# First mixer of a two-layer diffusion block: TensorE in a written order, each head's core in steps inside the next head's projection, scores in 32-wide pieces, conditioning ends put later

## Chip, cores and metric

One core of one Trainium2 chip. The metric is the device time of one execution in microseconds. TensorE does the matmuls (its weight loads are listed apart as PEld), VectorE (DVE) and ScalarE (ACT) work element by element, GpSimd (POOL) does a few small things, SyncE (SP) only issues transfers.

## What is computed

Two layers over 256 context and 256 latent tokens of width 1024. Each layer is a mixer and a mixture of 32 experts, both modulated by shifts, scales and gates that come from a conditioning vector. The first layer's mixer is a gated linear recurrence with 8 heads of 128, run forward and backward in chunks; the second's is attention. Cut to the part at hand:

```python
def gla_chunkwise(q, k, v, log_f, s0):          # per head, chunks of 32
    def step(s, blk):
        qc, kc, vc, gc = blk
        b = jnp.cumsum(gc, axis=-2)
        q_dec = qc * jnp.exp(b)
        scores = jnp.einsum('bhtc,bhsc->bhts', q_dec, kc * jnp.exp(-b))
        scores = jnp.where(lower_tri, scores, 0.0)
        o = scores @ vc + q_dec @ s             # and s_new from kc * exp(b_end - b), vc
    ...
def hgrn2_mixer(h_lat, h_ctx, ...):
    p = h @ w_in                                # q, z_fw, z_bw, v, g of 1024 each
    f = lb + (1 - lb) * sigmoid(z);  k = 1 - f;  log_f = log(f)
    ...                                         # context first, then latents; and both flipped
    return (rms_norm(o_fw + o_bw) * silu(g)) @ w_out

mod = silu(c) @ ada_w[i] + ada_b[i]             # six chunks of 1024: the conditioning
```

## The kernel before

The kernel is written in Python over a library that builds each engine's instruction list. Where nothing else is said, that library's planner sets the order on every engine: it takes the program's order as priority, its own cost estimate of each instruction and the buffers that come free, and puts on an engine what is ready. Inside a manual block for an engine, that engine keeps the order of the program; the others are still planned. Each engine then runs its list in order; waits between engines are semaphores.

`hgrn` (from L267) is the first mixer. All 512 tokens stand transposed as `hH` and `hL`, a high and a low part in a reduced fp32 format, so that a product of full precision is three matmuls. Weights arrive by SyncE in 2 MB (`slot`), are parted by `split` (L259) into `wH` (a ScalarE cast) and `wL` (a VectorE subtraction), three buffers each.

- Values (`vproj`, L378; `vstep`, L279): for heads 0 to 3 and again for heads 4 to 7, 96 matmuls into four accumulators; ScalarE copies them to `V4`. The second time is at head 4.
- Projections of a head (L506 to L523): four outputs q = 0 to 3 of 24 matmuls of 512 columns each (L513 to L515), one accumulator each: the two directions' gates, the query, the output gate. `dir_pre` (L393) turns a gate into `eq`, `ek`, `ke`, `kx` and `e` by a chain over ScalarE and VectorE with a scan; queries and output gates go through `sigmoid` (L176) and a product (L521).
- Conditioning: `ada_some(4)` (L373) puts four pieces behind each of the first six heads. A piece (`ada_piece`, L206) loads 1 MB of weights by SyncE into one of two buffers and multiplies it in four side-by-side 32-wide parts of the array (L212). Behind every eighth piece comes an end: the bias row, four transposes through the bank `sm` (L225), copies, and four small transfers by GpSimd (L242).
- Core of a head (`core`, L431): per direction `qm` and `qt` on VectorE, the scores (L450 with `ek`, 32 wide at a place of the array; L454 with `kx`, 64 wide), a masked copy (L456), three transposes of `ke` (L465), their copy `kT` on ScalarE (L467), three state products (L471), `S` (L473, L475); then the output (L487) of 20 instructions, its square sums, its norm (L494), four transposes (L498) and the gate (L499).

PSUM has eight banks: four rotating accumulators `mm` (projections, conditioning, router), one bank `sm` for all transposes and state products, one for the output, two for the scores. The order in the program is: the head's projection, its conditioning pieces, its core; the planner places the core's matmuls among the next head's projection. Behind head 7 come the router's small products (L606), the output projection (L558) and the routing; then the experts, whose weights (2 MB each) stream through the slots on SyncE's queue (L1029, L1032). The second layer's mixer, `mla`, runs sixteen more conditioning pieces by the same `ada_piece`.

Of the kernel before, what the change touches and what calls it, by code (L numbers as in the profile page):

```python
# [82 lines left out]
class K:  # L83
# [122 lines left out]
    def ada_piece(self, l, g, k, ps, w, tmp):  # L206
        nc, I = self.nc, self.I
        nc.sync.dma_start(w, I["ada_w"][l, g, k])
        if k == 0:
            self.ada_ps = ps()  # L210
        for a in range(4):
            nc.tensor.matmul(self.ada_ps[a * 32:(a + 1) * 32, :], self.cS[:, k, :], w[:, a * 512:(a + 1) * 512],  # L212
                             start=(k == 0), stop=(k == 7))
        if k < 7:
            return
        b, S, gf = tmp()
        (nc.scalar if l else nc.sync).dma_start(b, I["ada_b"][l, g])
        nc.vector.tensor_tensor(S, self.ada_ps, b, op=ALU.add)
        if g == 2:
            gf = gf[0:64]  # L220
            (nc.scalar if l else nc.sync).dma_start(gf, I["gffn"][l])
            nc.vector.scalar_tensor_tensor(S[0:64], S[0:64], 1.0, gf, op0=ALU.add, op1=ALU.mult)
# [44 lines left out]
    def hgrn(self):  # L267
        tc, nc, I = self.tc, self.nc, self.I
        PE, V, S, G = nc.tensor, nc.vector, nc.scalar, nc.gpsimd
        with ExitStack() as left, ExitStack() as st:  # L270
# [8 lines left out]
            def vstep(acc, k, H, L):  # L279
                c = slice(k % 2 * 512, k % 2 * 512 + 512)  # L280
                for tt in range(4):
                    ts = slice(tt * 128, tt * 128 + 128)
                    PE.matmul(acc[tt], hH[:, k, ts], H[:, c], start=(k == 0), stop=False)
                    PE.matmul(acc[tt], hH[:, k, ts], L[:, c], start=False, stop=False)
                    PE.matmul(acc[tt], hL[:, k, ts], H[:, c], start=False, stop=(k == 7))

            with tc.tile_pool(name="hin", bufs=1, side="right", reuse_waits="tile") as ip:
# [36 lines left out]
                for k in range(8):  # L324
                    if k % 2 == 0:
                        H, L = self.split(raw[:, k * 512:k * 512 + 1024], wp, [128, 1024])
                    vstep(acc, k, H, L)
# [41 lines left out]

            ada_todo = [(0, 1, k) for k in range(8)] + [(0, 2, k) for k in range(8)]  # L370
# [6 lines left out]

            def vproj(i, V4):  # L378

                acc_ = acc  # L380
                if i:
                    acc_, raw = [self.mm() for _ in range(4)], self.slot()
                    nc.sync.dma_start(raw, I["hg_wv"][i])
                    for q in range(4):
                        H, L = self.split(raw[:, q * 1024:(q + 1) * 1024], wp, [128, 1024])
                        for k in (2 * q, 2 * q + 1):
                            vstep(acc_, k, H, L)
                for tt in range(4):
                    S.copy(V4[:, tt, :], acc_[tt])

            v4 = lambda t: t.rearrange("p (t c j) -> p t c j", t=4, c=2)

            def dir_pre(h, d, z):  # L393
# [29 lines left out]
                ke = cw.tile([128, 512], F32, tag="ke", name="ke", bufs=2)  # L423
# [6 lines left out]

            def core(h, V4, hh, dd, sq, gs, dst):  # L431
                vs = slice(hh * 128, hh * 128 + 128)
                Sst, qts, scs = [], [], []
                both = cw.tile([128, 512], F32, tag="on", name="both")
                for d in range(2):
                    x = dd[d]
                    qm = x["eq"]
                    V.tensor_tensor(qm, sq, x["eq"], op=ALU.mult)
                    qt = cw.tile([128, 512], F32, tag="qt", name="qt", bufs=2)
                    V.tensor_tensor(v4(qt), v4(qm), x["sq"].to_broadcast([128, 4, 2, 64]), op=ALU.mult)  # L440
# [3 lines left out]
                    psc = scP[d]  # L444
                    for tt in range(4):
                        a = tt * 128
                        for c in range(4):
                            s0, c0 = a + c * 32, a + (c // 2) * 64
                            t0, n = (c0, 64) if c % 2 == d else (s0, 32)
                            PE.matmul(psc[c * 32:c * 32 + 32, t0:t0 + n], x["ek"][:, s0:s0 + 32], qm[:, t0:t0 + n],  # L450
                                      start=True, stop=True, tile_position=(0, c * 32))

                        t0 = a + 64 * (1 - d)
                        PE.matmul(psc[d * 64:d * 64 + 64, t0:t0 + 64], x["kx"][:, tt, :], qm[:, t0:t0 + 64], start=True, stop=True)  # L454
                    sc = scT[d]
                    V.copy_predicated(sc.rearrange("p (t j) -> p t j", t=4), masks[d].to_broadcast([128, 4, 128]),  # L456
                                      psc.rearrange("p (t j) -> p t j", t=4))
                    scs.append(sc)
                    if d:
                        V.tensor_tensor(both, scs[0], sc, op=ALU.add)  # L460
                    order = [0, 1, 2, 3] if d == 0 else [1, 0, 3, 2]
# [5 lines left out]
                    S.copy(kT, pk[:, 0:384])  # L467
                    pd = self.sm()
# [8 lines left out]
                    Sst.append((ss, {order[i + 1]: i for i in range(3)}))  # L477
                po = self.ac()
# [11 lines left out]
                for tt in range(4):  # L490
# [4 lines left out]
                                ssq.rearrange("p (t o) -> p t o", o=1).to_broadcast([128, 4, 128]), op=ALU.mult)  # L495
                pt = self.sm()
# [4 lines left out]
            for h in range(8):  # L501
                if h % 4 == 0:
                    V4 = cw.tile([128, 4, 512], F32, tag="V4", name="V4", bufs=2)
                    vproj(h // 4, V4)
# [3 lines left out]
                for q in range(4):  # L508
                    H, L = self.split(raw[:, q * 1024:(q + 1) * 1024], wp, [128, 1024])
                    p = self.mm()  # L510
                    for k in range(8):
# [3 lines left out]
                        PE.matmul(p, L[:, c], hH[:, k, :], start=False, stop=(k == 7))  # L515
                    if q < 2:
                        dd.append(dir_pre(h, q, p))
                    else:
# [3 lines left out]
                        if q == 2:  # L522
                            sq = t  # L523
                        else:
                            gs = t
                if h < 6:
                    ada_some(4)
                o7 = []

                def dst():  # L530
# [4 lines left out]
                if h == 5:  # L535
                    self.load_router(hp, 0)
                if h == 7:
                    self.router(hp, 0, self.mm())
                core(h, V4, h % 4, dd, sq, gs, dst)


# [991 lines left out]
```

## Time and profile before

| | us |
|---|---|
| runs of the kernel before | 1577.63, 1576.82, 1574.11 (median 1576.82) |
| the profiled execution | 1578.04 |
| its span, first to last instruction | 1576.3 |
| TensorE busy | 1499.6 (95%) |
| VectorE, ScalarE busy | 813.2 (52%), 449.1 (28%) |
| projections of heads 0 to 7, start to end | 53.1 to 344.7 |

The busy time of an engine is the time in which at least one of its instructions is under way. Matmuls are pipelined: a row's own duration reaches into the next one's, so a matmul's cost in a stream is the distance between two starts. The granted clock (PEclk) is the share of 2.4 GHz that TensorE was given; one half is 1.2 GHz.

### The profile page before, as it was taken

What the parts mean: (1) busy time and instruction counts of PE and PEld (TensorE: products, weight loads), DVE (VectorE), ACT (ScalarE), POOL (GpSimd) and SP (SyncE); (2) the same over time, 40 slices, a digit from 0 to 9 for tenths busy, and PEclk for the clock granted to TensorE, in tenths of its full rate; (3) what the DMA queues carried; (4) which work ended last, traced back from release to release, by engine and by line L of the source; (5) the groups of instructions that cost most, each with busy time, mean ns of one, the idle gap of its engine ahead of it and who ended that gap; (6) DMA issues with size and microseconds to landing.
All of it is one profiled execution on the core that took longest, in us unless ns stands there. A gap on an engine that the chain in (4) does not pass through costs nothing. (4 is left out here: it accounts for less than half of the span.)

```text
span 1576.3 us, 20139 instructions
## 1 busy us (share of the span) xinstructions
PE 1499.6 (95%) x8009; PEld 825.2 (52%) x8010; DVE 813.2 (52%) x1675; ACT 449.1 (28%) x938; POOL 74.9 (5%) x101
## 2 busy tenths in 40 slices
PE   7999999999899999999999999989799999998997
PEld 4777787778644544544544454447444443433433
DVE  5776647775824544544544567674534332332333
ACT  4554445553411111111111145554411111111110
POOL 0000000001300000000000011310100000000000
PEclk9999999999799999999999999999899999999999
DMA  9454534414769999999999957344799999999997
GB/s 384 165 201 177 196 136 161 188 54 161 276 240 399 429 428 426 428 427 426 427 429 423 356 218 305 141 187 142 272 392 428 427 427 428 428 427 428 427 425 268
DMA packets 63127, 500.80 MB, mean 318 GB/s; under 512 B 7024, under 2 KB 16624, under 8 KB 32816
## 3 DMA queue, kind: packets, MB, share of 16 engines
q1 hardware_dynamic: 59296, 490.87, 76.5%
q10 hardware_dynamic: 2816, 7.26, 1.4%
q0 software_dynamic: 912, 1.27, 0.3%
q8 instruction: 67, 1.10, 0.3%
q14 instruction: 36, 0.29, 0.0%
HBM read 498.26 MB, written 1.11 MB: 317 GB/s over the span
## 5 line engine op out<-in xcount | busy, mean ns | idle before, releaser
L1038 PE MATMUL mm<-w,xT 128*64 128x512 f32 x2048 | 469.9, 595 | 19.8 <-DMA w<-in_wg_dram 16.4
L1038 PEld LDWEIGHTS mm<-w,xT 128*64 128x64 f32 x2048 | 146.8, 137 | 310.7 <-issue 266.3
L1089 DVE TENSOR_TENSOR tmp<-p,rG 128x512 f32<-128x512 f32 (+1 forms) x106 | 68.0, 644 | 132.7 <-PE p L1087 132.6
L1090 DVE TENSOR_TENSOR x<-x,tmp 128x512 f32<-128x512 f32 (+1 forms) x195 | 132.4, 679 | 6.7
L1089 DVE TENSOR_TENSOR tmp<-p,x 128x512 f32<-128x512 f32 (+1 forms) x68 | 44.4, 655 | 165.1 <-PE p L1087 165.1
L1069 PE MATMUL mm<-w,x 128*64 128x512 f32 (+1 forms) x544 | 116.3, 570 | 1.6 <-ACT x L1057 1.4
L1069 PE MATMUL mm<-w,hT 128*64 128x512 f32 (+1 forms) x544 | 113.9, 570 | 1.4 <-ACT hT L1057 1.4
L889 PE MATMUL p<-sel,h2H 128*128 128x256 f32 x384 | 101.8, 300 | 1.8 <-DVE sel L879 1.8
L513 PE MATMUL mm<-hH,wH 128*128 128x512 f32 x256 | 101.9, 398 | 0.3 <-ACT wH L262 0.3
L515 PE MATMUL mm<-hH,wL 128*128 128x512 f32 x256 | 101.3, 396 | 0.5 <-DVE wL L264 0.5
L514 PE MATMUL mm<-hL,wH 128*128 128x512 f32 x256 | 100.6, 393 | 0.0
L890 PE MATMUL p<-sel,h2L 128*128 128x256 f32 x384 | 98.5, 290 | 0.0
L1076 DVE SCALAR_TENSOR_TENSOR yL<-mm,wsl,yH 128x512 fp32r<-128x512 f32 (+1 forms) x68 | 48.7, 716 | 71.6 <-ACT yH L1075 71.6
L1075 ACT ACTIVATE yH<-mm,wsl 128x512 fp32r<-128x512 f32 (+1 forms) x68 | 45.1, 663 | 123.3 <-PE mm L1069 93.2
L889 PEld LDWEIGHTS p<-sel,h2H 128*128 128x128 f32 x384 | 76.7, 200 | 5.1 <-issue 2.4
L264 DVE TENSOR_TENSOR wL<-w,wH 128x1024 fp32r<-128x1024 f32 x55 | 67.0, 1221 | 23.5 <-ACT wH L262 22.0
L1086 PE MATMUL p<-yH,G 128*128 128x512 f32 (+1 forms) x174 | 76.2, 441 | 0.9 <-DVE tmp L1089 0.9
L890 PEld LDWEIGHTS p<-sel,h2L 128*128 128x128 f32 x384 | 76.3, 199 | 1.4 <-issue 0.8
L1069 PEld LDWEIGHTS mm<-w,x 128*64 128x64 f32 x544 | 45.6, 137 | 60.0 <-issue 45.6
L262 ACT CAST wH<-w 128x1024 fp32r<-128x1024 f32 x55 | 57.3, 1047 | 63.3 <-PE mm L514 32.8
L1069 PEld LDWEIGHTS mm<-w,hT 128*64 128x64 f32 x544 | 37.5, 137 | 65.8 <-issue 59.7
L1086 PEld LDWEIGHTS p<-yH,G 128*128 128x128 f32 x174 | 32.5, 187 | 65.8 <-issue 51.5
(392 smaller groups left out, 2119.2 us busy)
## 6 DMA issues: line engine op xcount, KB each, us to landing
w<-in_wg_dram SPq DMA_DIRECT2D x52, 2048.0 KB, 18.1
w<-in_wu_dram SPq DMA_DIRECT2D x52, 2048.0 KB, 21.4
w<-in_wd_dram SPq DMA_DIRECT2D x52, 2048.0 KB, 20.2
aw<-in_ada_w_dram SPq DMA_DIRECT2D x32, 1024.0 KB, 6.0
w<-in_wd_dram SPq DMA_DIRECT2D x48, 512.0 KB, 8.7
w<-in_hg_w_dram SPq DMA_DIRECT2D x8, 2048.0 KB, 7.9
w<-in_wg_dram SPq DMA_DIRECT2D x32, 512.0 KB, 7.8
w<-in_wu_dram SPq DMA_DIRECT2D x32, 512.0 KB, 9.5
```

The lines of the kernel that those rows point to most:

```text
L262: nc.scalar.copy(H, raw)
L264: nc.vector.tensor_tensor(L, raw, H, op=ALU.subtract)
L513: PE.matmul(p, H[:, c], hH[:, k, :], start=(k == 0), stop=False)
L514: PE.matmul(p, H[:, c], hL[:, k, :], start=False, stop=False)
L515: PE.matmul(p, L[:, c], hH[:, k, :], start=False, stop=(k == 7))
L889: self.nc.tensor.matmul(o, self.h2H[:, tt, c], r, start=(tt == 0 and k == 0), stop=False)
L890: self.nc.tensor.matmul(o, self.h2L[:, tt, c], r, start=False, stop=(last and k == 1))
L1038: PE.matmul(p[a * 64:(a + 1) * 64, :], xT[:, k, a * 64:(a + 1) * 64], ws[a][:, k * 512:(k + 1) * 512], start=(k == 0), stop=(k == 7))
L1069: PE.matmul(p[a * 64:(a + 1) * 64, :], hT[:, j, a * 64:(a + 1) * 64], ws[a][:, j * 1024 + n * w_:j * 1024 + n * w_ + w_], start=(j == 0), ...
L1086: PE.matmul(pc, g, yH, start=True, stop=False)
L1089: V.tensor_tensor(t, pc, rG[vec(tt)][:, ns], op=ALU.mult)
L1090: adder.tensor_tensor(x[:, tt, ns], x[:, tt, ns], t, op=ALU.add)
```

## The change

TensorE gets a manual block over the loop of the heads. Projections, value projection and core become generators; `beside` runs a projection in 32 steps of three matmuls and takes the next step of the previous head's core behind steps 7, 10, 12, 17, 19, 22 and 30. Conditioning pieces come in pairs behind steps 7 and 21; an end that is left over comes behind step 5 of the next job. The scores of both directions come together, and the `kx` products are cut from 64 to 32 wide. `ke` has three buffers in place of two. The bias row is asked for at piece 5 (in the second layer's later groups at piece 5 and again at piece 7).

```diff
@@ ada_piece
+        if k == 5 or (l == 1 and g and k == 7):
+            self.ada_tmp = b, S, gf = tmp()
+            (nc.scalar if l else nc.sync).dma_start(b, I["ada_b"][l, g])
+            if g == 2:
+                (nc.scalar if l else nc.sync).dma_start(gf[0:64], I["gffn"][l])
         if k < 7:
             return
-        b, S, gf = tmp()
-        (nc.scalar if l else nc.sync).dma_start(b, I["ada_b"][l, g])
+        b, S, gf = self.ada_tmp
         nc.vector.tensor_tensor(S, self.ada_ps, b, op=ALU.add)
...
+        if l == 1 and g:
+            self.ada_tail(l, g, S)
+        else:
+            self.ada_left = l, g, S
+
+    def ada_tail(self, l, g, S):
...
@@ vstep
                     PE.matmul(acc[tt], hL[:, k, ts], H[:, c], start=False, stop=(k == 7))
+                    yield
...
-                ke = cw.tile([128, 512], F32, tag="ke", name="ke", bufs=2)
+                ke = cw.tile([128, 512], F32, tag="ke", name="ke", bufs=3)
...
+            def scores(dd, qms):
+                for tt in range(4):
+                    a = tt * 128
+                    for d in range(2):
+                        for c in range(4):
+                            s0, c0 = a + c * 32, a + (c // 2) * 64
+                            t0, n = (c0, 64) if c % 2 == d else (s0, 32)
+                            PE.matmul(scP[d][c * 32:c * 32 + 32, t0:t0 + n], dd[d]["ek"][:, s0:s0 + 32], qms[d][:, t0:t0 + n],
+                                      start=True, stop=True, tile_position=(0, c * 32))
+                    for c in range(4):
+                        d = c // 2
+                        t0 = a + 64 * (1 - d)
+                        PE.matmul(scP[d][c * 32:c * 32 + 32, t0:t0 + 64], dd[d]["kx"][:, tt, c % 2 * 32:c % 2 * 32 + 32],
+                                  qms[d][:, t0:t0 + 64], start=True, stop=True, tile_position=(0, c * 32))
+
+            def core(h, V4, dd, sq, gs, dst):
+                for d in range(2):
+                    qm = dd[d]["eq"]
+                    V.tensor_tensor(qm, sq, qm, op=ALU.mult)
+                    qms.append(qm)
+                yield
+                scores(dd, qms)
+                ...             # qt, masked copies, both
+                for d in range(2):
+                    yield
+                    ...         # transposes of ke, kT
+                    yield
+                    ...         # state products, S
+                yield
+                ...             # output, square sums, norm
+                yield
+                ...             # four transposes, gate
...
-                        PE.matmul(psc[d * 64:d * 64 + 64, t0:t0 + 64], x["kx"][:, tt, :], qm[:, t0:t0 + 64], start=True, stop=True)
...
+            def beside(job, side, ada=False):
+                next(side, None)
+                for i, _ in enumerate(job, 1):
+                    if i == 5 and self.ada_left:
+                        self.ada_tail(*self.ada_left)
+                        self.ada_left = None
+                    if ada and i in (7, 21):
+                        ada_some(2)
+                    if i in (7, 10, 12, 17, 19, 22, 30):
+                        next(side, None)
+
+            V4, side = values(acc), iter(())
+            with tc.manual_schedule(engines={mybir.EngineType.PE}):
+                for h in range(8):
+                    if h == 4:
+                        res = []
+                        beside(vproj(res), side)
+                        V4, side = res[0], iter(())
+                    res = []
+                    beside(project(h, res), side, h < 6)
+                    side = core(h, V4, *res, dst_of(h))
+                    if h == 5:
+                        self.load_router(hp, 0)
+            self.router(hp, 0, self.mm())
+            for _ in side:
+                pass
```

## Rows read from the trace of the kernel before

**Rows 1.** The page: busy time of the engines, and the span in 40 equal slices (39.4 us each), busy share in tenths, for TensorE and for the transfers.
```profile
PE 1499.6 (95%) x8009; PEld 825.2 (52%) x8010; DVE 813.2 (52%) x1675; ACT 449.1 (28%) x938; POOL 74.9 (5%) x101
...
PE   7999999999899999999999999989799999998997
...
DMA  9454534414769999999999957344799999999997
```
**Rows 2.** Busy time of each engine by stretches: the projections of heads 0 to 7, the last head of them, the tail of the mixer, and most of the first expert stage. Columns: stretch, its length, then busy us and instructions of TensorE, its weight loads, VectorE, ScalarE and GpSimd, the granted clock, the transfers' share and GB/s.
```profile
53.13:344.68 291.55, 289.57 (x1922) 216.47 (x1922) 203.39 (x376) 151.74 (x301) 5.77 (x22) 1.00 0.42 159
313.35:346.25 32.90, 31.99 (x233) 25.56 (x234) 25.14 (x48) 18.98 (x39) 0.04 (x1) 1.00 0.17 65
346.25:412.14 65.89, 62.08 (x363) 50.54 (x364) 42.42 (x93) 24.76 (x50) 13.64 (x15) 0.95 0.39 134
480.00:900.00 420.00, 419.32 (x2083) 194.79 (x2081) 202.35 (x323) 45.79 (x83) 0.00 (x0) 1.00 1.01 422
```
**Rows 3.** TensorE's timeline around the end of head 1's projection: start, duration, line, operation, result and operands, weights' and moving shapes, count. Between the first two rows lie 67 more projection matmuls; the conditioning matmuls (L212), the scores (L450, L454) and the next projection follow.
```profile
95.63 0.39 PE L513 MATMUL mm<-hH,wH 128*128 128x512 f32 x1
...
111.06 0.39 PE L515 MATMUL mm<-hH,wL 128*128 128x512 f32 x1
111.38 1.92 PE L212 MATMUL mm<-aw,cS 128*32 128x512 f32 x16
113.12 0.29 PE L450 MATMUL p<-eq,ek 128*32 128x64 f32 x8
113.34 0.33 PE L454 MATMUL p<-eq,kx 128*64 128x64 f32 x2
113.59 0.31 PE L450 MATMUL p<-eq,ek 128*32 128x64 f32 x8
...
117.13 0.50 PE L513 MATMUL mm<-hH,wH 128*128 128x512 f32 x1
...
119.53 0.39 PE L514 MATMUL mm<-hL,wH 128*128 128x512 f32 x1
119.84 1.07 PE L212 MATMUL mm<-aw,cS 128*32 128x512 f32 x8
120.84 0.49 PE L487 MATMUL p<-V,both 128*128 128x128 f32 x2
121.08 0.47 PE L515 MATMUL mm<-hH,wL 128*128 128x512 f32 x1
121.40 0.39 PE L513 MATMUL mm<-hH,wH 128*128 128x512 f32 x1
```
**Rows 4.** The 64-wide score matmuls of the window from 53.13 to 344.68 us, grouped by line and shape: count, busy us together, mean ns of one, idle time before them.
```profile
L454 PE MATMUL p<-eq,kx 128*64 128x64 f32 x112 | 18.4, 246 | 0.0
```
**Rows 5.** Timelines of TensorE, ScalarE and VectorE over the core of head 5 (transposes, copy, state products, the two copies and updates of the state, output, the projection that goes on behind it, cast of the next weights, transposes).
```profile
321.74 0.49 PE L465 MATMUL p<-ident,ke 128*128 128x128 f32 x3
...
322.79 0.94 PE L471 MATMUL p<-V,kT 128*128 128x128 f32 x6
...
324.08 0.49 PE L487 MATMUL p<-S,qt 128*128 128x128 f32 x2
...
326.12 0.48 PE L513 MATMUL mm<-hH,wH 128*128 128x512 f32 x1
...
331.40 0.63 PE L498 MATMUL p<-ident,on 128*128 128x128 f32 x4
...
322.26 0.48 ACT L467 COPY kT<-p 128x384 f32<-128x384 f32 x1 [3.04 <-PE p L465]
...
327.77 1.03 ACT L262 CAST wH<-w 128x1024 fp32r<-128x1024 f32 x1
...
324.06 0.73 DVE L475 SCALAR_TENSOR_TENSOR S<-S,e,p 128x128 f32<-128x128 f32 x2 [2.14 <-ACT S L473]
```
**Rows 6.** Timelines of TensorE, VectorE and ScalarE where head 3's projection ends and the second value projection (L283) begins; L521 is the last reader of the fourth projection accumulator, L182 one of the three ScalarE steps of the sigmoid before it.
```profile
183.24 1.92 PE L212 MATMUL mm<-aw,cS 128*32 128x512 f32 x16
...
188.99 0.50 PE L283 MATMUL mm<-wH,hH 128*128 128x512 f32 x1
...
188.72 0.68 DVE L521 TENSOR_TENSOR sq<-sq,mm 128x512 f32<-128x512 f32 x1
...
186.49 0.63 ACT L182 ACTIVATE sq<-sq 128x512 f32<-128x512 f32 x1
```
**Rows 7.** Transfers: the conditioning weights on SyncE's queue (count, size, median us from issue to landing), and the bias rows of the second layer on ScalarE's (duration of an issue in ns, least, median and most, first and last start).
```profile
aw<-in_ada_w_dram SPq DMA_DIRECT2D x32, 1024.0 KB, 6.0
...
L217 ACTq DMA_DIRECT2D w<-in_ada_b_dram x2: 338/343/348, 933.5 to 968.9; - x2
```
**Rows 8.** Waits of SyncE's queue from 340 to 480 us: who waited for whom, us in total, times, longest.
```profile
SPq L1029 <- DVE wL L264: 75.4, 2, 43.4
```
**Rows 9.** All engines' timeline at the start of a conditioning pair (weight loads and matmuls of L212), and the weight loads of the `ek` products from 53.13 to 344.68 us by shape.
```profile
111.38 0.16 PEld L212 LDWEIGHTS mm<-aw,cS 128*32 128x32 f32 x8 [0.35 <-issue]
111.38 1.06 PE L212 MATMUL mm<-aw,cS 128*32 128x512 f32 x8
...
111.83 0.13 PEld L212 LDWEIGHTS mm<-aw,cS 128*32 128x32 f32 x4 [0.30 <-issue]
...
L450 PEld LDWEIGHTS p<-eq,ek 128*32 128x32 f32 x448 | 9.2, 108 | 8.8 <-DVE eq L438 4.0 <-issue 1.6 <-DVE ke L428 0.3
```
**Rows 10.** Waits in the window from 53.13 to 344.68 us: the casts of weights that waited for TensorE to leave a buffer.
```profile
ACT wH L262 <- PE mm L514: 32.8, 15, 9.4
```

More of the change, by code (lines that the diff above doesn't have):

```diff
@@ L326, in hgrn @@
                         H, L = self.split(raw[:, k * 512:k * 512 + 1024], wp, [128, 1024])
-                    vstep(acc, k, H, L)
+                    for _ in vstep(acc, k, H, L):
+                        pass
             self.dump("hT", hH)
@@ L376, in ada_some, with values, vproj @@
                                    lambda: [hp.tile([128, 512], F32, tag="adx", name=f"ad{t}", bufs=4) for t in "bsg"])
[L378 to L387, printed above, removed]
+            def values(acc_):
+                V4 = cw.tile([128, 4, 512], F32, tag="V4", name="V4", bufs=2)
                 for tt in range(4):
                     S.copy(V4[:, tt, :], acc_[tt])
+                return V4
+            def vproj(res):
+                acc_, raw = [self.mm() for _ in range(4)], self.slot()
+                nc.sync.dma_start(raw, I["hg_wv"][1])
+                for q in range(4):
+                    H, L = self.split(raw[:, q * 1024:(q + 1) * 1024], wp, [128, 1024])
+                    for k in (2 * q, 2 * q + 1):
+                        yield from vstep(acc_, k, H, L)
+                res.append(values(acc_))
             v4 = lambda t: t.rearrange("p (t c j) -> p t c j", t=4, c=2)
@@ L429, in dir_pre @@
                 return dict(eq=eq, ek=ek, ke=ke, kx=kx, sq=sq_, E=e)
-            def core(h, V4, hh, dd, sq, gs, dst):
-                vs = slice(hh * 128, hh * 128 + 128)
-                Sst, qts, scs = [], [], []
+            def scores(dd, qms):
[13 more added lines that the diff above has]
+            def core(h, V4, dd, sq, gs, dst):
+                vs = slice(h % 4 * 128, h % 4 * 128 + 128)
+                orders = [[0, 1, 2, 3], [1, 0, 3, 2]]
+                Sst, qts, qms = [], [], []
+                for d in range(2):
[4 more added lines that the diff above has]
+                scores(dd, qms)
                 both = cw.tile([128, 512], F32, tag="on", name="both")
@@ L436, in core @@
                     x = dd[d]
-                    qm = x["eq"]
-                    V.tensor_tensor(qm, sq, x["eq"], op=ALU.mult)
                     qt = cw.tile([128, 512], F32, tag="qt", name="qt", bufs=2)
-                    V.tensor_tensor(v4(qt), v4(qm), x["sq"].to_broadcast([128, 4, 2, 64]), op=ALU.mult)
+                    V.tensor_tensor(v4(qt), v4(qms[d]), x["sq"].to_broadcast([128, 4, 2, 64]), op=ALU.mult)
                     second = v4(qt)[:, :, 1 - d, :]
@@ L443, in core @@
                     qts.append(qt)
[L444 to L453, printed above, removed]
-                        PE.matmul(psc[d * 64:d * 64 + 64, t0:t0 + 64], x["kx"][:, tt, :], qm[:, t0:t0 + 64], start=True, stop=True)
[L455 to L461, printed above, removed]
+                for d in range(2):
+                    V.copy_predicated(scT[d].rearrange("p (t j) -> p t j", t=4), masks[d].to_broadcast([128, 4, 128]),
+                                      scP[d].rearrange("p (t j) -> p t j", t=4))
+                V.tensor_tensor(both, scT[0], scT[1], op=ALU.add)
+                for d in range(2):
+                    x, order = dd[d], orders[d]
+                    yield
                     pk = self.sm()
@@ L499, in core, with project @@
                 V.scalar_tensor_tensor(dst(), pt, self.cols[:, 64:65], gs, op0=ALU.mult, op1=ALU.mult)
[L501 to L504, printed above, removed]
+            def project(h, res):
                 dd = []
@@ L515, in hgrn @@
                         PE.matmul(p, L[:, c], hH[:, k, :], start=False, stop=(k == 7))
+                        if k < 7:
+                            yield
                     if q < 2:
@@ L521, in hgrn, with dst_of @@
                         V.tensor_tensor(t, t, p, op=ALU.mult)
[L522 to L528, printed above, removed]
+                        res.append(t)
+                    if q == 3:
+                        res.insert(0, dd)
+                    yield
+            o7 = []
+            def dst_of(h):
                 def dst():
@@ L534, in dst @@
                     return o7[0]
[L535 to L539, printed above, removed]
+                return dst
+            def beside(job, side, ada=False):
[3 more added lines that the diff above has]
+                        self.ada_tail(*self.ada_left)
+                        self.ada_left = None
+                    if ada and i in (7, 21):
[16 more added lines that the diff above has]
+            for _ in side:
+                pass
             wop = [self.slot() for _ in range(2)]
```

5 lines of the change are left out of this document (2 added, 3 removed).

## Prediction, made before the changed kernel was run

> **What bounds the kernel now.** I read the page first, for engine shares by slice, and see TensorE at nine tenths or more nearly everywhere, while the transfers are only half busy in the first quarter and full in the two expert stages [rows 1]. Then the windows by stage: from the first head's projection to the end of the eighth, TensorE is busy 289.57 of 291.55 us, VectorE 203.39, ScalarE 151.74, the transfers 0.42 of the time [rows 2]. So this mixer is bound by TensorE and there are almost no holes to fill: 1.98 us of idle time in all. A reordering can win little by itself; what can win is a TensorE instruction that takes less time. So the next view is the timeline of TensorE in one head, by starts, because busy times overlap there (a projection matmul is booked at 0.39 us and the next one starts 0.227 us later: 69 of them from 95.63 to 111.06) [rows 3].
>
> In that timeline one block is slow for its size: the scores. From 113.12 to 117.13 is 4.01 us for matmuls of 32 or 64 columns [rows 3]. Its pattern repeats eight times in about 0.50 us: four products of `ek` (eight instructions, one 32-wide piece of the array each) start within 0.22 us, then the product of `kx`, 64 wide, takes 0.25 us (113.34 to the next four) [rows 3]. The 64-wide one spans two pieces and starts only when the four before it are through; the four behind it wait for it in turn. Seven heads of this lie in the mixer's window: 112 instructions on `kx`, 16 a head [rows 4].
>
> **The change, part by part.** The sum is made against the profiled execution, 1578.04 us (1576.3 of span and 1.7 around it); the median of the runs shown is 1576.82, 1.2 lower, and the last step takes that off.
>
> *Scores.* The 64-wide products become pairs of 32-wide ones: per tile of 128 tokens 12 products of 32 columns' weights, all in the same four pieces, three rounds of four in place of two rounds and two wide products. What a piece then has to stream per tile is 64+32+64 = 160 columns in two passes. The conditioning matmuls show the speed of such pieces without any wide one between: 16 instructions of 512 columns, four side by side, in 1.74 us, so four passes of 0.434 us, or 0.85 ns a column and pass [rows 3]. 160 x 2 x 0.85 = 0.27 us a tile, 1.09 for the four tiles of a head, if each piece ran on its own. Starts are in order across the pieces, and the 32-column products then stand behind 64-column ones; three full rounds of 64 are 64 x 3 x 2 x 0.85 = 0.33 us a tile, 1.31 a head; with about 0.15 to drain into the next kind of work it is 1.5 us, which I take. Bounds: 1.2 below; above, each round of four still drained before the next, as the first four are today, 12 x 0.22 = 2.64 us. The gain is 4.01 - 1.5 = 2.5 us a head, eight heads: **-20.1 us** (the eighth behind the projections, where TensorE is still busy 62.08 of 65.89 us [rows 2]).
>
> *Conditioning pieces.* Now each head's four come as one pair (1.74 us) and two singles at 1.00 us each [rows 3]; then as two pairs. 2.00 - 1.74 less 0.1 for the way back to a projection is 0.16, six heads: **-1.0 us**. The ends taken out (four transposes) are the same number and move by a few microseconds; the VectorE copies and four small GpSimd transfers of each end go with them and are wanted only after the mixer, so nothing (bounds 0 and 0.5 if the copies hold the bank that they share with the head's steps).
>
> *Cuts.* Each place where the projection is interrupted costs 0.1 to 0.25 us over its matmuls (119.53 to 119.84 is 0.31, and 121.08 to 121.40 is 0.32, where 0.227 is usual) [rows 3]. The written order has seven to nine cuts a head; today's order has about as many. Nothing, with +-0.2 x 2 x 7 = 3 us as bounds.
>
> *Today's idle time.* Of the 1.98 us I count **-1.4 us** back, as waits for a product placed too early, and keep 0.6 for the start of the first projection (bounds 0 and 1.98).
>
> *Hand-offs.* From here the order can't bend. The steps stand at 7, 10, 12, 17, 19, 22 and 30 of 32 projection steps of 3 x 0.227 = 0.68 us. Transposes to state products (10 to 12, 17 to 19): about 0.25 + 1.36 = 1.6 us apart. Today 1.05 us do without a visible wait: transposes 321.74, copy on ScalarE 322.26 for 0.48, products 322.79 [rows 5]. The 0.56 us of slack does not cover a 1.03 us cast of weights that stands in front of the copy [rows 5]. ScalarE is 58% busy (18.98 of 32.90 us) [rows 2]; I take 0.2 us at each of 14 places: **+2.8 us** (bounds 0 and 0.7 each, 10 us). State products to output: three steps and the products' own 0.7 give 2.7 us (4.5 where a conditioning pair lies between); today 1.29 us pass (322.79 to 324.08), part of it the copy and the two updates on VectorE (until 324.79) [rows 5]. Output to its transposes: the output's own 2.04 (324.08 to 326.12) + 8 x 0.68 = 7.5 us, against 7.3 today [rows 5]; **+0.7 us** for seven heads, bounds 0 and 4. The scores themselves need both directions' `eq`; they are ready before step 7, 4.8 us into the projection, today they are used 2 us into it [rows 3]: nothing.
>
> *The second value projection.* It takes all four rotating accumulators at once, and runs directly behind head 3's projection. The last of the four is still read by the gate's sigmoid: today that read ends at 188.72 + 0.68 = 189.4 [rows 6], 6.2 us after the projection's end at 183.2, covered by a conditioning pair and the scores, so that the value products start at 188.99 [rows 6]. In the written order those come at step 7 and the fourth accumulator is wanted after three short steps, 2.0 us. The chain alone (one VectorE step at 0.68, three of ScalarE at 0.63, one of VectorE at 0.68 [rows 6]) is 3.3 us before any way between engines, with queues 5. **+2.5 us** (bounds 1.5 and 4.2).
>
> *Transfers.* On SyncE's queue a pair's two loads are issued when the pair before has left its buffers, 14 steps (9.5 us) or more ahead of use, against 6.0 us to land [rows 7]; the heads' 2 MB loads stand in that queue too, but a head ahead. The bias rows are asked for two pieces earlier. The transfers are 0.42 busy from 53 to 345 us [rows 2], so all this is nothing (bounds 0 and 3, if one head's load lands between a pair's two). In the second layer, though, the condition asks at piece 5 and again at piece 7: three transfers twice, on ScalarE's queue at 0.34 us an issue [rows 7], in a stage that I have no reason to call bound by ScalarE: **+0.4 us**, bounds 0 and 3 (if ScalarE holds for the first copy to land).
>
> Sum: -20.1 - 1.0 - 1.4 + 2.8 + 0.7 + 2.5 + 0.4 = **-16.1 us**. 1578.04 - 16.1 = 1561.9, on the runs' scale 1561.
>
> *Does it arrive at the end?* The expert stage from 480 us is full of transfers (1.01 of the time, 422 GB/s [rows 2]), so its length can't shrink; but its stream is started by buffers. The weight loads' longest waits before it, 75.4 us in two, are for the split of the output projection's weights [rows 8], work that follows the mixer on TensorE. So the whole stage shifts.
>
> **Rivals.** *A: rounds still drain.* If a piece can't take its next product before the round of four is through, a head's scores take 2.64 us and the gain is 11.0 instead of 20.1: 1570. For it: the gap before `kx` today. Against: in the conditioning rounds the same pieces follow each other at the pace of the columns.
>
> *B: weight loads come into the open.* If a load of weights can't run beside the products of the same piece, each of 24 passes a head adds its 0.108 us [rows 9]: 2.6 us, scores as long as now, and the sum is 1582, slower. Against it: in the conditioning rounds the eight loads of the first two passes are all issued within 0.16 us from 111.38, and the next four at 111.83, so the loads of the second pass run while the matmuls of the first do [rows 9]. The Trainium skill, "TensorE: Matmul & The Clock Gate", in the section on packing small matmuls by row and column tiling, says that a weight load overlaps matmuls under way only when their row groups differ; here all rows are in use, so by that rule B would be the forecast. The trace does not agree: loads of the same rows overlap at 111.38.
>
> *C: TensorE held at the hand-offs*, the case on the slow side. The place is the copy on ScalarE and the updates on VectorE between a head's steps, five hand-offs a head, 35 in the window. A cast of weights (1.03 us) in front, with what is left of it when the copy becomes ready and the way there and back, is about 0.7 us over the slack; casts already wait for TensorE to free their buffers, 32.8 us in 15 waits [rows 10], and hold what stands behind them. At 0.7 everywhere it is 24.5 us in place of the 3.5 in the sum: 1582. It decides from an average of 0.64 us; at 0.55 the change is worth nothing. Against it: today's order has shorter distances at the same places and 1.98 us of idle time in all.
>
> *D: given back.* The expert stream starts no earlier, or the mixer's end finds the clock low: 1577. Against: the waits before that stream are on the mixer's work [rows 8]. The clock is a swing of its own: after the mixer 0.05 of 65.89 us is lost to half clock [rows 2], 3.3 us that may be there or not.
>
> **How the numbers follow.** Forecast, 1561, own range 1550 to 1567: chance 0.69. A, 1570: 0.17. D: 0.05. C: 0.07. B: 0.02. Two in a thousand, 3.2 us, is about what a measurement of this kernel tells from no change. The forecast and A are faster, D is the same, B and C are slower: 0.86, 0.05, 0.09. The range goes from 1550 (no hand-off cost, 3.5, scores at 1.2 us, 2.4, fewer cuts, 2, and the clock's 3.3) to 1574 (A and the clock's 3.3); C, D and B lie outside with 0.14.
>
> **What would show it.** Right: a head's scores from first to next kind of work in about 1.5 us and no 64-wide `kx`; conditioning only in pairs; the mixer's window some 14 us shorter and the rest unchanged in length but shifted; 2 to 3 us of TensorE idle at the start of the second value projection, on an accumulator. Wrong: scores above 2.2 us (A) or near 4 (B); idle time of TensorE at state products or transposes over 10 us, ended by ScalarE or VectorE (C); weight stream of the experts starting at today's time (D).

## The result, and the profile after

The changed kernel takes 1561.83 us (median of 4 runs, 1560.77 to 1562.05) against 1576.25 for the kernel before: ratio 0.9905, interval 0.9893 to 0.9917. Forecast were 1561 and a range of 1550 to 1574. The profiled execution is 1562.05 us, 16.0 less than the 1578.04 of before; the sum was -16.1. Medians and ratios in this document leave out two executions that stand far apart from all others, 3774 us of `e7_copy_closer` and 1705 us of the kernel before.

The page after, lines that answer to [rows 1]:
```profile
span 1560.4 us, 20387 instructions
...
PE 1476.0 (95%) x8137; PEld 816.6 (52%) x8138; DVE 811.0 (52%) x1675; ACT 446.6 (29%) x938; POOL 74.5 (5%) x101
...
PE   7999999999799999999999999989899999998997
```
The shares say nothing: TensorE is at 95% before and after. The stretches, as in [rows 2] (the projections of the eight heads; the tail of the mixer; the expert stage; the second layer's mixer up to its experts):
```profile
53.28:331.75 278.47, 270.39 (x2037) 207.71 (x2038) 202.65 (x379) 149.95 (x301) 5.76 (x22) 0.99 0.44 167
331.68:395.86 64.18, 58.63 (x400) 47.82 (x400) 43.87 (x96) 25.91 (x52) 13.36 (x15) 0.98 0.42 148
480.00:880.00 400.00, 399.33 (x1980) 184.01 (x1978) 190.37 (x302) 44.18 (x79) 0.00 (x0) 1.00 1.01 423
880.90:1102.70 221.80, 199.91 (x1044) 116.59 (x1042) 148.50 (x417) 114.55 (x295) 44.27 (x43) 0.98 0.55 208
```
The window of the projections is 13.08 us shorter (291.55 to 278.47) and carries 82% of the 16 us. But its idle time on TensorE rose from 1.98 to 8.08 us: more was won than arrived. The scores of one head on TensorE's timeline, to be held against [rows 3]:
```profile
120.39 0.36 PE L457 MATMUL p<-eq,ek 128*32 128x64 f32 x16
120.56 0.30 PE L462 MATMUL p<-eq,kx 128*32 128x64 f32 x8
120.67 0.36 PE L457 MATMUL p<-eq,ek 128*32 128x64 f32 x16
120.85 0.30 PE L462 MATMUL p<-eq,kx 128*32 128x64 f32 x8
...
121.42 0.30 PE L462 MATMUL p<-eq,kx 128*32 128x64 f32 x8
121.65 0.50 PE L543 MATMUL mm<-hH,wH 128*128 128x512 f32 x1
```
A head takes 1.26 us in place of 4.01, a tile 0.28 (120.39 to 120.67) in place of 1.00; the other six heads of the window take 1.26 to 1.29. Seven heads: 7 x 2.75 = 19.2 us less; with 6.1 us more idle time that leaves 13.1, all of the window. What TensorE waited for there:
```profile
PE p L501 <- ACT kT L496: 5.1, 6, 0.9
PE mm L293 <- DVE sq L553: 2.4, 1, 2.4
PE mm L545 <- DVE wL L274: 0.5, 1, 0.5
PE mm L543 <- ACT wH L272: 0.3, 1, 0.3
```
Two new waits, both at places that the prediction named. The first, at the second direction's state products, six heads of seven (the timelines of TensorE and of ScalarE, as [rows 5]):
```profile
129.68 0.52 PE L494 MATMUL p<-ident,ke 128*128 128x128 f32 x3
...
132.44 0.94 PE L501 MATMUL p<-V,kT 128*128 128x128 f32 x6 [0.85 <-ACT kT L496]
...
130.47 1.04 ACT L272 CAST wH<-w 128x1024 fp32r<-128x1024 f32 x1
131.41 0.62 ACT L181 ACTIVATE s<-s 128x512 f32<-128x512 f32 x1
131.94 0.45 ACT L496 COPY kT<-p 128x384 f32<-128x384 f32 x1
```
The transposes are through at about 130.2; the copy stands behind a cast of weights and a step of the next sigmoid and starts at 131.94. The second wait, at the second value projection (TensorE and VectorE, as [rows 6]):
```profile
181.82 0.39 PE L295 MATMUL mm<-wH,hL 128*128 128x512 f32 x1
184.59 0.57 PE L293 MATMUL mm<-wH,hH 128*128 128x512 f32 x1 [2.39 <-DVE sq L553]
184.96 0.63 PE L294 MATMUL mm<-wL,hH 128*128 128x512 f32 x1
185.38 0.63 PE L295 MATMUL mm<-wH,hL 128*128 128x512 f32 x1
...
183.85 0.68 DVE L553 TENSOR_TENSOR sq<-sq,mm 128x512 f32<-128x512 f32 x1
```
After three short steps the fourth accumulator is still read by the gate until 184.53. The matmuls behind the wait start 0.42 us apart instead of 0.227: half clock for 3.4 us (the granted clock is 0.54 from 184.59 to 188.00). Behind the mixer all comes earlier by the same amount: the second layer's mixer ends its stretch at 1102.70 us in place of 1119.30, and is as long as before (221.80 and 221.74 us). The weight loads' longest waits, to be held against [rows 8], still end at the output projection's split:
```profile
SPq L1085 <- DVE wL L274: 76.2, 2, 44.7
```
The stretch of the second layer's mixer in the kernel before:
```profile
897.56:1119.30 221.74, 201.43 (x1041) 117.21 (x1042) 148.97 (x417) 114.62 (x295) 44.30 (x43) 0.97 0.55 206
```

### The profile page after: what moved, and what is told of

Read it like the earlier page. It is cut to its first block, busy times and chain, and to the rows that moved or that the text cites. A ratio compares the mean times of both kernels' runs of the same rounds, so it can differ in the third digit from the quotient of the medians.

```text
span 1560.4 us, 20387 instructions
## 1 busy us (share of the span) xinstructions
PE 1476.0 (95%) x8137; PEld 816.6 (52%) x8138; DVE 811.0 (52%) x1675; ACT 446.6 (29%) x938; POOL 74.5 (5%) x101
## 5 line engine op out<-in xcount | busy, mean ns | idle before, releaser
L1094 PE MATMUL mm<-w,xT 128*64 128x512 f32 x2048 | 471.6, 597 | 19.2 <-DMA w<-in_wg_dram 15.4
L1094 PEld LDWEIGHTS mm<-w,xT 128*64 128x64 f32 x2048 | 150.2, 137 | 308.9 <-issue 263.6
L543 PE MATMUL mm<-hH,wH 128*128 128x512 f32 x256 | 105.1, 411 | 0.3 <-ACT wH L272 0.3
```

What stands on the lines that cost most here:

```text
L543: PE.matmul(p, H[:, c], hH[:, k, :], start=(k == 0), stop=False)
L1094: PE.matmul(p[a * 64:(a + 1) * 64, :], xT[:, k, a * 64:(a + 1) * 64], ws[a][:, k * 512:(k + 1) * 512], start=(k == 0), stop=(k == 7))
```

## The experiments

Two theories stood against each other first. **W**, width: the narrow score pieces are the gain, and the written order wins nothing net. **O**, order: the steps wide apart are the gain. Ratios are to the kernel before on the same chip; "window" and "idle" are the stretch of the eight projections and TensorE's idle time in it, from one profile each.

| kernel | median us | ratio, 95% interval | window, idle us |
|---|---|---|---|
| changed, again (`e0_after`) | 1562.35 | 0.9912, 0.9893 to 0.9931 | 276.48, 8.2 |
| `e1_narrow_only` | 1564.97 | 0.9926, 0.9905 to 0.9948 | 282.25, 4.9 |
| `e2_wide_in_order` | 1570.58 | 0.9957, 0.9943 to 0.9970 | 285.14, 8.2 |
| `e3_planned` | 1556.43 | 0.9873, 0.9852 to 0.9894 | 272.29, 3.9 |
| `e4_fourth_later` | 1557.65 | 0.9875, 0.9859 to 0.9890 | 274.03, 5.7 |
| `e5_ask_once` | 1563.27 | 0.9900, 0.9884 to 0.9916 | 277.99, 8.2 |
| `e6_copy_wider` | 1561.25 | 0.9896, 0.9880 to 0.9912 | 279.16, 6.6 |
| `e7_copy_closer` | 1566.20 | 0.9928, 0.9913 to 0.9943 | 279.60, 11.1 |
| `e8_joint_narrow` | 1565.32 | 0.9927, 0.9909 to 0.9946 | 282.62, 8.2 |
| `e9_order_mended` | 1552.21 | 0.9852, 0.9830 to 0.9874 | 271.22, 2.9 |
| `e10_mended_planned` | 1555.27 | 0.9862, 0.9840 to 0.9884 | 272.32, 3.9 |

**The changed kernel again.** 

> The changed kernel itself, on the chip of the next three, as their yardstick. 1562 us, 0.990 to 0.992 of the kernel before on either theory.

It came out so. Its profile has the same two waits (5.1 and 2.4 us), but no half clock behind the second:
```profile
52.32:328.80 276.48, 268.32 (x2034) 206.36 (x2034) 202.23 (x378) 149.84 (x300) 5.78 (x22) 1.00 0.45 168
...
183.63 0.50 PE L293 MATMUL mm<-wH,hH 128*128 128x512 f32 x1 [2.38 <-DVE sq L553]
183.97 0.39 PE L294 MATMUL mm<-wL,hH 128*128 128x512 f32 x1
```
So the drop after that wait is not sure to come; most of the 2 us between the windows of two profiles of one kernel is this. The same wait of 2.4 us stands in the profiles of `e2_wide_in_order`, `e5_ask_once`, `e6_copy_wider` and `e7_copy_closer`; the half clock follows in the first three and not in the last. With this it followed in four of six profiles, so single windows of these kernels can differ by some 2 us for this reason.

**Narrow pieces alone.**
```diff
-                        PE.matmul(psc[d * 64:d * 64 + 64, t0:t0 + 64], x["kx"][:, tt, :], qm[:, t0:t0 + 64], start=True, stop=True)
+                        for c in (2 * d, 2 * d + 1):
+                            PE.matmul(psc[c * 32:c * 32 + 32, t0:t0 + 64], x["kx"][:, tt, c % 2 * 32:c % 2 * 32 + 32],
+                                      qm[:, t0:t0 + 64], start=True, stop=True, tile_position=(0, c * 32))
```


> The kernel before, with its 64-wide kx products cut into two 32-wide ones at their places in the array and nothing else; the planner keeps the order. Theory W (width): the gain is the narrow pieces; in the changed kernel a head's scores take 1.26 us in place of 4.01, and the written order pays back what it wins (0.85 us of waiting at six state products, 2.4 us and a half clock at the second value projection). Here the two directions still come one after the other, so a head takes 1.5 to 2.0 us: 7.5 heads x 2.0 to 2.5 = 15 to 19 us less than before, 1557 to 1561 us. Theory O (order): the gain is the written order with its wide steps; narrow pieces alone leave the cuts and the waits, 1568 to 1573 us.

11.7 us less by the ratio (0.9926), between the two: width has most of the gain, not all that W gave it. TensorE's timeline of one head's scores:
```profile
112.49 0.28 PE L450 MATMUL p<-eq,ek 128*32 128x64 f32 x7
112.56 0.22 PE L455 MATMUL p<-eq,kx 128*32 128x64 f32 x1
...
114.10 0.28 PE L455 MATMUL p<-eq,kx 128*32 128x64 f32 x2
114.31 0.50 PE L515 MATMUL mm<-hH,wH 128*128 128x512 f32 x1
```
1.82 us here and in the two other heads that run without a cut; the mean of seven is 2.1, as four are cut by other work and partly wait. The `kx` products start among the `ek` ones (112.56): a piece goes on as soon as it is free and doesn't wait for the others. One direction's `kx` falls on two pieces only. An estimate from the pace of 0.85 ns a column and pass: the busiest piece has 128 columns a tile, 0.87 us a direction, 1.74 a head, near the 1.82 and above 1.26.

**Wide pieces in the written order.**
```diff
-                    for c in range(4):
-                        d = c // 2
+                    for d in range(2):
                         t0 = a + 64 * (1 - d)
-                        PE.matmul(scP[d][c * 32:c * 32 + 32, ...
+                        PE.matmul(scP[d][d * 64:d * 64 + 64, t0:t0 + 64], dd[d]["kx"][:, tt, :], qms[d][:, t0:t0 + 64],
```


> The changed kernel with the kx products 64 wide again, two per tile behind the two rounds of ek, everything else (written order, both directions together) as it is. Theory W: each tile changes from 32 to 64 wide and back once, which costs 0.15 us each way beside the products: 0.6 to 0.8 us a tile, 2.4 to 3.2 us a head against 1.26; plus 9 to 16 us on the changed kernel, 1571 to 1578 us. Theory O: the order keeps its gain, at most plus 5: 1562 to 1567 us.

8 us over the changed kernel, just short of W's span and outside O's. A head:
```profile
121.89 0.36 PE L457 MATMUL p<-eq,ek 128*32 128x64 f32 x16
122.18 0.34 PE L461 MATMUL p<-eq,kx 128*64 128x64 f32 x4
122.45 0.38 PE L457 MATMUL p<-eq,ek 128*32 128x64 f32 x16
...
124.18 0.50 PE L542 MATMUL mm<-hH,wH 128*128 128x512 f32 x1
```
2.29 us, 0.56 a tile: with both directions together the width changes once a tile and back, not twice. The two wide products, at different halves of the array, take 0.27 us (122.18 to 122.45) where one took 0.25 (113.34 to 113.59 in [rows 3]), so they run side by side. The four cases, uncut heads, are 4.01 (wide, apart), 1.82 (narrow, apart), 2.29 (wide, together), 1.26 (narrow, together). A tile is 0.26 us longer by wide products when there is one change and back, 0.55 when there are two: the cost goes with the change of width, about 0.26 to 0.28 us there and back, and not with the wide product.

**The same program, planned.**
```diff
-            with tc.manual_schedule(engines={mybir.EngineType.PE}):
+            with ExitStack():
```


> The changed kernel without the manual block: same program, same narrow pieces, but the planner sets TensorE's order as on the other engines. Theory W: the order as such is worth little either way; without it the waits at the state products and at the second value projection go (6 x 0.85 + 2.4 + 1.7 for the half clock = 9 us) and the planner's cuts and early products come back (about 3 to 6 us): 1556 to 1562 us. Theory O: plus 8 to 14 us, 1570 to 1576 us.

W's span, at its low end: 0.9873 against 0.9912, 6 us less than the changed kernel, with the same 1.26 a head. So the manual block itself cost about 6 us; 4.2 of them show in the window, and TensorE's idle time there is 4.3 us less.
```profile
53.01:325.30 272.29, 268.37 (x2034) 206.39 (x2034) 201.85 (x379) 150.37 (x301) 5.79 (x22) 1.00 0.45 171
...
PE p L501 <- ACT kT L496: 2.4, 6, 0.4
PE p L530 <- DVE on L525: 1.0, 2, 0.5
```
The wait at the values is gone, that at the state products halved; two waits before the output's transposes, 1.0 us together, are new.

**The fourth accumulator later.**
```diff
-                    for k in (2 * q, 2 * q + 1):
-                        yield from vstep(acc_, k, H, L)
+                    for tts in ((0, 1, 2), (3,)):
+                        for k in (2 * q, 2 * q + 1):
+                            yield from vstep(acc_, k, H, L, tts)
```


> The changed kernel with the second value projection taking its fourth accumulator after six short steps in place of three (token tiles 0 to 2 for both halves of a quarter, then tile 3). Theory P (accumulator): TensorE's 2.39 us of idle time there is the gate's sigmoid still reading that accumulator; with 2.0 us more ahead of it the idle time falls to 0.3 to 0.5, the rest is unchanged: 2 us less (3.7 where the half clock that followed in one trace goes too), 1558 to 1561 us against 1562. Theory Q (queue): VectorE simply comes to the gate late and later still when TensorE runs on: the idle time stays near 2 us, 1562 us.

Theory P: the first step on the fourth accumulator, the seventh of the short steps, starts without a wait (183.60), and the window is 2.45 us shorter than in `e0_after`.
```profile
183.31 0.40 PE L295 MATMUL mm<-wH,hL 128*128 128x512 f32 x1
183.60 0.50 PE L293 MATMUL mm<-wH,hH 128*128 128x512 f32 x1
```
Its median is 4.7 us lower. Neither of the two profiles compared has the half clock that follows this wait in four of six; where it comes, it goes with the wait, and that may be part of what lies beyond 2.45. It was not traced.

**Rows asked for once.**
```diff
-        if k == 5 or (l == 1 and g and k == 7):
+        if k == 5:
```


> The changed kernel with the bias and norm rows of the second layer asked for once, at piece 5, and not again at piece 7. Theory S (small): three transfers less on ScalarE's queue, nothing waits on them for long: 0 to 1 us less, 1561 to 1562 us, inside what can be told. Theory L (landing): ScalarE or VectorE holds for the second copy to land: 2 to 4 us less, seen in the attention's stretch.

Nothing to be told in the time (0.9900), so theory S. What theory L named is there all the same: in the changed kernel ScalarE twice holds for a row asked for again, 4.1 and 3.5 us (from the view of the line that asks: who waited for it), and here it doesn't.
```profile
ACT w L1469: 4.1, 1
ACT w L266: 3.5, 1
```
It cost nothing that shows at the end: the second layer's stretch of 221.80 us is 223.72 here, at a lower granted clock (0.95, and 0.98 there).

**The second state products at step 20.**
```diff
-                    if i in (7, 10, 12, 17, 19, 22, 30):
+                    if i in (7, 10, 12, 17, 20, 22, 30):
```


> The changed kernel with the second direction's state products at step 20 in place of 19, three steps behind their transposes. Theory H (hand-off): the 0.85 us that TensorE waits at six of seven heads for the copy on ScalarE, which stands behind a cast of weights (1.03) and a step of a sigmoid (0.62), is a fixed distance in time; 0.68 us more of it leaves 0.17 each: 6 x 0.68 = 4.1 us less waiting, at most 0.5 given back where the output then comes two steps behind without a conditioning pair between (two heads): 1558 to 1559 us against 1562. Theory R (moves along): ScalarE's queue moves with TensorE, the wait stays near 0.85: 1562 us.

The wait fell as theory H said, from 5.1 to 1.1 us, and the time by no more than noise (1561.25 against 1562.35):
```profile
130.75 0.71 PE L501 MATMUL p<-V,kT 128*128 128x128 f32 x4 [0.16 <-ACT kT L496]
...
297.53 0.63 PE L530 MATMUL p<-ident,on 128*128 128x128 f32 x4 [1.87 <-DVE on L525]
298.71 0.63 PE L543 MATMUL mm<-hH,wH 128*128 128x512 f32 x1
```
In the projection of head 6, which carries no conditioning pair, the output's norm now comes too late for its transposes: 1.87 us, and matmuls 0.43 us apart, half clock, from 298.71 on for 3.4 us. Another 0.5 us is waited for `eq`. One hand-off's slack was taken from another's. That this profile's window is longer than that of `e0_after` is also the half clock behind the wait at the values, which `e0_after` has not.

**One step closer.**
```diff
-                    if i in (7, 10, 12, 17, 19, 22, 30):
+                    if i in (7, 10, 11, 17, 18, 22, 30):
```


> The changed kernel with both directions' state products one step closer to their transposes (11 and 18 in place of 12 and 19). Theory H: the second direction's wait grows by 0.68 to 1.53 us at six heads, plus 4.1 us; the first direction's copy is ready 1.01 us behind its transposes where the products then come after 0.93: 0.1 to 0.4 each, plus 1 to 3 us. 5 to 7 us more waiting, 1567 to 1569 us. Theory R: under 2 us more, 1562 to 1564 us.

```profile
PE p L501 <- ACT kT L496: 8.1, 6, 1.4
```
Each wait is 1.35 in place of 0.85, so 0.5 of the 0.68 came through; at the first direction's products there is no wait. By medians it is 3.9 us more than `e0_after`, of which 3.0 are these waits. Theory H, but with less than its 5 to 7 us of waiting.

**Joint narrow scores in the old program.** Both `qm` first, then the changed kernel's `scores`, the rest of the old `core` behind:
```diff
+                for d in range(2):
+                    qm = dd[d]["eq"]
+                    V.tensor_tensor(qm, sq, qm, op=ALU.mult)
+                    qms.append(qm)
+                ...                      # the scores of the changed kernel
                 for d in range(2):
+                    x, qm = dd[d], qms[d]
-                    for tt in range(4):
-                        ...              # the scores of one direction
```


> The kernel before with the changed kernel's scores (both directions of a tile together, three rounds of four 32-wide pieces) and nothing else: singles and pairs of conditioning, ends, projections and the planner's order stay. Theory J (joint scores): narrow pieces one direction at a time took 2.09 us a head, together they take 1.3; 8 x 0.79 = 6.3 us less than the narrow-only kernel's 0.9926, so 0.988 to 0.990, about 1558 to 1561 on the scale of 1577. Theory S (steps): most of the 8.5 us between the narrow-only kernel and the planned one comes from the program written in steps (pairs, wide distances as priorities); then at most 2 us of it come here, 0.991 to 0.993.

Theory J fails: 0.9927, no better than narrow alone; theory S's span holds it. A head's scores take 1.26 us where they have what they need (148.13 to 149.39), but the old program puts them right behind the projection, before both directions' `qm`:
```profile
148.13 0.36 PE L446 MATMUL p<-eq,ek 128*32 128x64 f32 x16
...
149.39 0.44 PE L471 MATMUL p<-ident,ke 128*128 128x128 f32 x2
...
53.26:335.88 282.62, 274.43 (x2033) 205.97 (x2034) 201.71 (x375) 151.91 (x300) 5.76 (x22) 1.00 0.44 164
...
PE p L446 <- DVE eq L438: 2.5, 5, 0.9
PE p L493 <- DVE both L466: 2.0, 2, 1.0
PE mm L283 <- DVE sq L527: 1.3, 1, 1.3
```
So the program written in steps is worth something after all: 0.9927 here, 0.9873 in `e3_planned`, with the same scores and no manual block in either. Of the 10.3 us between their windows, 4.3 are idle time and 6.1 are busy time of TensorE (274.43 against 268.37).

**The written order mended.** The edits of `e4_fourth_later` and `e5_ask_once`, and
```diff
-                    if i in (7, 10, 12, 17, 19, 22, 30):
+                    if i in (7, 10, 12, 17, 20 if ada else 19, 22, 30):
```


> The written order with three menders: the fourth value accumulator later, the second state products at step 20 only in projections that carry conditioning pairs (four heads), the second layer's rows asked for once. Hand-off theory: 2.4 us less waiting at the values, 4 x 0.68 = 2.7 less at the state products, nothing from the rows: 0.986 to 0.987, level with the planned kernel (0.9873). If waits only move along: 0.9875 or more, as the kernel with the fourth accumulator alone.

```profile
53.21:324.43 271.22, 268.33 (x2034) 206.35 (x2034) 201.75 (x378) 149.79 (x300) 5.76 (x22) 1.00 0.45 171
...
PE p L502 <- ACT kT L497: 2.3, 6, 0.8
```
A little below the forecast's low end: the fastest kernel here, 25.8 us under the kernel before by the medians on its chip. Step 20 where a pair follows takes its 0.68 four times and nothing is late behind it: the window is 2.8 us shorter than that of `e4_fourth_later`.

**Mended, but planned.** The same as `e9_order_mended` but with step 19 everywhere and `ExitStack()` for the manual block. 

> The planned kernel (no manual block) with the fourth value accumulator later and the second layer's rows asked for once. The planner had no wait at the values to begin with, so both should do nothing: 0.986 to 0.9885, as the planned kernel alone (0.9873). If the later accumulator helps the planner as it helped the written order: 0.984 to 0.986.

0.9862: as the planned kernel. The menders help only the written order, and with them it and the planner can't be told apart (the intervals overlap).

## Why the prediction was right, and where it was not

*Scores*, -20.1: the step held. Seven heads brought -19.2; the eighth lies behind the window, where the rest of the gain, 2.9 us, arrived; the forecast had 2.5 there for this head. That share is not shown: the clock granted in the mixer's tail differs too, 0.95 in the 65.89 us of [rows 2] and 0.98 in the 64.18 us after, which is an estimated 2.0 us by itself. The size was off by 0.24 us a head: I held the starts in order across the pieces and took 1.5, but a piece goes on by itself (112.56 in `e1_narrow_only`), and a tile takes 0.28, the 0.27 that the pure columns gave. Rival A (drained rounds, 2.64) and rival B (open weight loads, near 4) are excluded by 1.26. The Trainium skill, "TensorE: Matmul & The Clock Gate", section on packing small matmuls by row and column tiling, lets a weight load overlap matmuls under way, in its list of what overlaps, only where their row groups differ. The runs here don't agree for column pieces over all rows: by that rule a head would have stayed near 4 us, and it takes 1.26. The same section, above that list, also lets a load go ahead into a background weight buffer, and that would fit what is seen here.

*Hand-offs*, +2.8: the step named the place and the cause, a cast in front of the copy, and mis-sized it. It is 5.1 us: 0.85 at six of the second direction's places, above the bound of 0.7, and nothing at the first's, not 0.2 at 14. In front of the copy stood a step of a sigmoid beside the cast. The share by which ScalarE is busy was the wrong measure; its queue stands in the same order in every head, and the wait came at the same place in each of the six. Output to transposes, +0.7: 0.1.

*The second value projection*, +2.5: 2.39, by the accumulator named, and `e4_fourth_later` took it away.

*Conditioning pairs* -1.0, *cuts* 0, *idle time* -1.4: of the window's 13.08 us, scores and the new idle time leave nothing, but the half clock's 1.7 us (half of the 3.4) are in the same remainder. In `e0_after`, which has no half clock there, the window is 15.1 us shorter, scores 19.2 less 6.2 of idle time give 13.0, and 2.0 us are left: pairs and cuts together won about that, in place of 1.0. Which of them did is not shown. Of the idle time of before, 0.8 us stayed (the two last rows of the waits) and 1.2 went, counted in the 6.1 and 6.2.

*Rows asked for twice*, +0.4: 221.80 us for that stretch, 221.74 before; nothing at the end, though ScalarE held for them, and `e5_ask_once` is no faster.

*Arrival at the end*: held; rival D is out.

*Rival C* was the mechanism at two places, not the outcome: 7.5 us, where it needed 22. (B's 1582 is on the profile's scale; on the runs' scale it is 1581.)

That the sum came within 0.1 us is in part luck. The hand-offs cost 2.3 us more than forecast and the half clock 1.7; the scores (1.7 better over seven heads), the output's transposes, the rows, and the pairs and cuts paid for it. Two profiled executions of the changed kernel differ by 1.2 us (1562.05 and 1560.82).

What the prediction put wrongly in words: that a reordering can win little by itself. Against narrow scores alone (0.9926), the steps with mended distances reach 0.9852, 11.7 us more, and so they do against joint narrow scores in the old order (0.9927). So it is the order of the program, planned or written; taking the scores together wins nothing without it, as they then wait for `qm`. What in the steps does it (the pairs, the distances, the third buffer of `ke`, the later ends) was not taken apart.

## What to carry to other kernels

Where TensorE is full, look for an instruction that is slow for its size: here each change from 32-wide to 64-wide pieces and back cost about 0.27 us, twice a tile, and either cutting the wide ones (4.01 to 1.82 us) or grouping them (to 2.29) was worth about half of the time. An order written by hand wants each hand-off longer than the other engine's queue, worst item first; widen it where other work already stands between, since elsewhere the slack comes out of the next hand-off (step 20 everywhere took 4.0 us of waiting away and brought 2.4 back elsewhere; before conditioning pairs only, 2.8 us came through in the window). Having written the steps, also let the planner order them: it takes the program's order as its priority, and here did as well.

## What the runs showed of the hardware

Four 32-wide pieces of the array run on their own, each at 0.85 ns a column and pass, and a product of one may start before another piece's earlier product is through. A change from 32-wide to 64-wide pieces and back cost about 0.27 us. A wait of 2.4 us on TensorE in full work was followed by a stretch at 1.2 GHz in four of six profiles (3.4 us in the changed kernel's) and by none in two, one of them of the same kernel.
